# The final RMSNorm of a hybrid decoder step: its factors with tokens on the partitions, formed by a power on GpSimd

## The chip, the cores and the metric

The kernel runs on one core of a Trainium2 chip. The metric is the device time of one execution in microseconds, as a median over several runs. One execution was also taken by the hardware profiler; "the span" is the time from its first to its last instruction.

The five engines are named as in the profile: PE (TensorE, with PEld for its weight loads), DVE (VectorE), ACT (ScalarE), POOL (GpSimd) and SP (SyncE, which here only issues DMAs). Each works through its own queue in order and waits for the others through semaphores.

## The reference, cut to what matters

One layer of a decoder, for 512 prompt tokens and 8 sample tokens of 1024 features, in float32: dilated attention and a gated linear attention, then an MLP with a squared ReLU, then a last norm. The end is what the change touches:

```python
def rmsnorm(x, g):
    xf = x.astype(jnp.float32)
    y = xf * lax.rsqrt(jnp.mean(xf * xf, axis=-1, keepdims=True) + EPS)
    return (y * g.astype(jnp.float32)).astype(x.dtype)
...
    h = x + mix @ w_o
    f = jnp.square(jax.nn.relu(rmsnorm(h, g_norm2) @ w_up))
    return h + f @ w_down
...
    y_prompt = rmsnorm(xp, g_final)
    y_sample = rmsnorm(xs, g_final)
```

## The kernel before

Activations lie with features on the 128 partitions and tokens along the free dimension: a tile `B` is [128, 8, 520], 8 feature blocks by 520 tokens (512 prompt and 8 sample tokens, in two column halves of 260). Weights come as panels of 128 output features by 8 blocks of 128 input features. To keep float32 accuracy with the faster float32r matmuls, every operand is split into a high part and a low part (hi by ScalarE's Copy, lo by a subtraction on VectorE), and each product takes three passes: hi x hi, hi x lo, lo x hi (`passes`, `split_panel`, line 90 and 91). One panel is thus 8 x 3 x 2 = 48 matmuls of 128x128 weights against 260 columns, in `panel_mms` (line 124).

The order of the work on each engine is set when the program is built: a scheduler places the instructions of each engine by a simulated timeline, and PSUM banks and tiles are handed out in rotation. On the chip each engine keeps that order.

The MLP runs in four quarters of the hidden width (`qd`). In each quarter eight `w_up` panels give f, the squared ReLU, split into `fh` and `fl` (lines 982 to 986): ReLU on ScalarE into `relu`, then max(ps, 0) x relu on VectorE into `fsq`, then the split. Then eight `w_down` panels are summed into `dd`. The norm ahead of the MLP is not applied to its input. Its square, `rv` = 1 / (mean + eps), is applied behind the squared ReLU instead, since relu(s x)^2 = s^2 relu(x)^2 for a positive s. For the first three quarters `dd` is multiplied by `rv` and added to `H` in the last quarter's up loop (lines 988 and 989).

The last quarter's `w_down` product is written out by hand, with its eight panels kept in SBUF (tiles `lw`), once for each column half j (0 and 1): for each of the 8 output blocks k, 24 matmuls into a bank `mps` (line 1017), then `xo` = mps x rv (line 1020), dd += xo (line 1021), the square of dd (line 1023, ACT), the running sum of squares `acc` (line 1025, all but the last square), and dd times the final norm's weight (line 1026, ACT). Behind the eight blocks come the half's norm factors: a sum over the partitions by a matmul with a matrix of ones, for `acc` (line 1028) and for the last square (line 1029), which leaves the sum on every partition; then `rsqrt` (lines 184 to 189): Ln and Exp on ScalarE and one Newton step on VectorE, on 128x260 each; then four products of two blocks each with the factors (line 1034) and their DMAs to `yT` (line 1036).

The banks `mps`, `r2`, `r3` of this part come from a pool of four PSUM banks (`bank`). On GpSimd's queue stand 42 DMAs that copy the attention caches to the outputs (line 167), paced by the matmuls.

Of the kernel before, what the change touches and what calls it, by code (L numbers as in the profile page):

```python
# [9 lines left out]
F32 = mybir.dt.float32  # L10
F32R = mybir.dt.float32r
U8 = mybir.dt.uint8
AF = mybir.ActivationFunctionType
ALU = mybir.AluOpType
# [4 lines left out]
D = 1024  # L19
S = 512  # L20
NB = 8
P = 128
HC = 260
NT = 2 * HC
KT = 8
EPS = 1e-6
# [14 lines left out]
def halves(t):  # L41
    return t.rearrange("p (j c) -> p j c", j=2)


class Build:
# [751 lines left out]
    def run(self):  # L797
        nc, tc, I, O = self.nc, self.tc, self.I, self.O
# [56 lines left out]
        p = aps.enter_context(pool("ap"))  # L855
# [73 lines left out]
        with pool("late") as p:  # L929
            for x in range(2):  # L930
                for k, ps in enumerate(self.panel_mms(oah, oal, 4), 4 * x):
                    ga = halves(gA[:, k])
                    for o, i in ((ga[:, 0], ps[0]), (ga[:, 1], ps[1])) if isinstance(ps, list) else ((ga, ps),):
                        nc.vector.tensor_tensor(o, i, o, op=ALU.mult)
            mh, ml = self.big("mh", F32R), self.big("ml", F32R)
            H = self.big("H")
            nc.sync.dma_start(H, I["xT"])
            for k in range(KT):
                ps = self.panel_mm(obh, obl)
                nc.vector.tensor_tensor(halves(gB[:, k]), ps, halves(gB[:, k]), op=ALU.mult)  # L940
                nc.vector.tensor_tensor(gA[:, k], gA[:, k], gB[:, k], op=ALU.add)
                nc.scalar.activation(mh[:, k], gA[:, k], AF.Copy)
                nc.vector.tensor_tensor(ml[:, k], gA[:, k], mh[:, k].bitcast(F32), op=ALU.subtract)
                self.pace(1)
            hh, hl = self.big("hh", F32R), self.big("hl", F32R)
            acc = p.tile([P, NT], F32, tag="acc", name="acc")
            for k in range(KT):
                ps = self.panel_mm(mh, ml)
                nc.vector.tensor_tensor(halves(H[:, k]), ps, halves(H[:, k]), op=ALU.add)
                nc.scalar.activation(hh[:, k], H[:, k], AF.Copy, scale=self.g("n2", k))  # L950
                nc.vector.scalar_tensor_tensor(hl[:, k], H[:, k], self.g("n2", k), hh[:, k].bitcast(F32),
                                               op0=ALU.mult, op1=ALU.subtract)
                if k == 0:
                    nc.scalar.activation(acc, H[:, k], AF.Square)
                else:
                    sq = p.tile([P, NT], F32, tag="sq", name="sq", bufs=2)
                    nc.scalar.activation(sq, H[:, k], AF.Square)
                    nc.vector.tensor_tensor(acc, acc, sq, op=ALU.add)
                self.pace(1)
            rv = p.tile([P, NT], F32, tag="rv", name="rv")  # L960
            self.rawp, self.rawb = p, 3
            fh, fl = self.big("fh", F32R), self.big("fl", F32R)
            dd = self.big("dd")
            for qd in range(4):
                if qd == 3:
                    flat = lambda t: t.rearrange("p a b -> p (a b)")[:, :4 * D].rearrange("p (i k n) -> p i k n", i=4, k=KT)
                    n0 = len(self.panels) - KT
                    wd = [[flat(self.big(f"lw{x}", F32R)) for x in range(2)]]
                for k in range(KT):
                    if qd == 3 and k == KT - 1:  # L970
                        for i in range(4):
                            self.wdst[n0 + i] = (wd[0][0][:, i], wd[0][1][:, i])
                    ps = self.panel_mm(hh, hl)
                    if qd == 0 and k == 0:
                        for j in range(2):
                            pr = self.bank("r2")
                            nc.tensor.matmul(pr[:, :HC], self.ones, acc[:, j * HC:(j + 1) * HC], start=True, stop=True)
                            nc.vector.tensor_scalar(rv[:, j * HC:(j + 1) * HC], pr[:, :HC], 1 / D, EPS,
                                                    op0=ALU.mult, op1=ALU.add)
                        nc.vector.reciprocal(rv, rv)  # L980
                    t = p.tile([P, NT], F32, tag="relu", name="relu", bufs=2)
                    nc.scalar.activation(halves(t), ps, AF.Relu)
                    f = p.tile([P, NT], F32, tag="fsq", name="fsq", bufs=2)
                    nc.vector.scalar_tensor_tensor(halves(f), ps, 0.0, halves(t), op0=ALU.max, op1=ALU.mult)
                    nc.scalar.activation(fh[:, k], f, AF.Copy)
                    nc.vector.tensor_tensor(fl[:, k], f, fh[:, k].bitcast(F32), op=ALU.subtract)
                    if qd == 3:
                        nc.vector.tensor_tensor(dd[:, k], dd[:, k], rv, op=ALU.mult)
                        nc.vector.tensor_tensor(dd[:, k], dd[:, k], H[:, k], op=ALU.add)
                    self.pace(1)  # L990
                if qd == 3:
                    break
                for k in range(KT):
                    ps = self.panel_mm(fh, fl)
                    dv = halves(dd[:, k])
                    if qd == 0:
                        nc.vector.tensor_copy(dv, ps)
                    else:
                        nc.vector.tensor_tensor(dv, ps, dv, op=ALU.add)
                    self.pace(1)  # L1000
            self.pace(1000)
            wd.append([flat(self.big(f"lw{2 + x}", F32R)) for x in range(2)])
            for i in range(4):
                self.wdst[n0 + 4 + i] = (wd[1][0][:, i], wd[1][1][:, i])
            for j in range(2):
                cc = slice(j * HC, (j + 1) * HC)
                for k in range(KT):
                    i = n0 + k
                    if j == 0:
                        if i + 2 < len(self.panels):  # L1010
                            self.load_panel(i + 2)
                        if i + 1 < len(self.panels):
                            self.split_panel(i + 1)
                    ps = self.bank("mps")[:, :HC]
                    for kk in range(KT):
                        for n, (w, x) in enumerate(self.passes(self.split[i], kk, fh, fl)):
                            nc.tensor.matmul(ps, w, x[:, kk, cc], start=(kk == 0 and n == 0),  # L1017
                                             stop=(kk == KT - 1 and n == 2))
                    t = p.tile([P, NT], F32, tag="relu", name="xo", bufs=2)[:, :HC]
                    nc.vector.tensor_tensor(t, ps, rv[:, cc], op=ALU.mult)  # L1020
                    nc.vector.tensor_tensor(dd[:, k, cc], dd[:, k, cc], t, op=ALU.add)
                    sq = p.tile([P, NT], F32, tag="sq", name="sq", bufs=2)[:, :HC]
                    nc.scalar.activation(sq if k else acc[:, cc], dd[:, k, cc], AF.Square)
                    if 0 < k < KT - 1:
                        nc.vector.tensor_tensor(acc[:, cc], acc[:, cc], sq, op=ALU.add)
                    nc.scalar.activation(dd[:, k, cc], dd[:, k, cc], AF.Copy, scale=self.g("fin", k))
                pr = self.bank("r3")
                nc.tensor.matmul(pr[:, :HC], self.ones, acc[:, cc], start=True, stop=False)
                nc.tensor.matmul(pr[:, :HC], self.ones, sq, start=False, stop=True)
                rs = p.tile([P, HC], F32, tag="rs3", name="rs3", bufs=2)  # L1030
                self.rsqrt(p, rs, pr[:, :HC], HC, 1 / D)
                for k in range(0, KT, 2):
                    ks = slice(k, k + 2)
                    nc.vector.tensor_tensor(dd[:, ks, cc], dd[:, ks, cc], rs.unsqueeze(1).to_broadcast([P, 2, HC]),
                                            op=ALU.mult)
                    nc.sync.dma_start(O["yT"][:, ks, cc], dd[:, ks, cc])

# [145 lines left out]
```

## Time and profile before

| | us |
|---|---|
| median of 3 runs | 938.59 (937.89 to 943.15) |
| profiled execution | 939.2 |
| its span | 937.4 |
| PE busy | 920.3 (98% of the span), 8306 matmuls |
| DVE, ACT, POOL busy | 549.0, 380.0, 67.4 |

In a row of a timeline or chain the first number is the start in us from the span's start, the second the duration in us. In a row of groups, "x4 | 0.8, 198" is the count, the busy time in us and the mean duration in ns. A busy PE is not a PE at its peak, since matmuls overlap: the busy time of one matmul in a stream is longer than its distance to the next. Idle time in brackets names the engine whose work ended the wait.

### The profile page before, as it was taken

Reading aid. Unit: us, or ns where it says so; the run is one execution under the profiler, and the core shown is the slowest. Engines: PE = TensorE matmul, PEld = TensorE weight load, DVE = VectorE, ACT = ScalarE, POOL = GpSimd, SP = SyncE. Lnnn points to the kernel's source line nnn. Section 1 sums busy time; section 2 is a strip of 40 time slices with the busy share of each in tenths; the row PEclk is TensorE's granted clock in tenths of the full one; section 3 lists DMA queues with packets and bytes.
Section 4 is the critical chain, followed back from the end, with each engine's and each line's share of the span. In section 5 each row is a group of like instructions: output and inputs, shape, how many; then the busy total and the mean of one; then the engine's idle time right before and its main releaser. Section 6 shows DMA issues by size and latency. Waiting matters only on the chain.

```text
span 937.4 us, 19831 instructions
## 1 busy us (share of the span) xinstructions
PE 920.3 (98%) x8306; PEld 896.3 (96%) x8306; DVE 549.0 (59%) x1078; ACT 380.0 (41%) x735; POOL 67.4 (7%) x119
## 2 busy tenths in 40 slices
PE   9899999999999999999999999999999999999995
PEld 9899999999998999989999999999999999999995
DVE  7757566665766949586855556433443345555654
ACT  6133423443645536565633443322432243224432
POOL 1000000000201112010000000010000000000000
PEclk9899999999999999999999999999999999999998
DMA  6365454233444444222677767777865232323301
GB/s 245 114 237 181 142 191 155 101 131 116 166 150 165 128 165 144 69 74 69 235 278 277 272 226 269 270 269 270 294 254 175 96 93 87 104 92 106 121 30 63
DMA packets 37147, 155.27 MB, mean 166 GB/s; under 512 B 5129, under 2 KB 11537, under 8 KB 35106
## 3 DMA queue, kind: packets, MB, share of 16 engines
q1 hardware_dynamic: 32066, 95.26, 29.8%
q0 software_dynamic: 4848, 58.73, 18.0%
q8 instruction: 65, 1.06, 0.5%
q14 instruction: 24, 0.20, 0.1%
q10 hardware_dynamic: 144, 0.01, 0.0%
HBM read 140.66 MB, written 54.17 MB: 208 GB/s over the span
## 4 chain that ended last, share of the span: by engine, by line
PE 95%; DVE 2%; DMA 1%; issue 1%; ACT 0%; SPq 0%; DVEq 0%; ACTq 0%
PE mps L124 80%; PE mps L1017 5%; PE pvp L383 1%; PE lev L583 1%; PE gpo L670 1%; PE vps L318 1%; PE ptp L368 1%; PE gpu L674 1%; PE sps L352 1%; DMA xr<-in_xT 1%; PE gso L737 1%; PE gpo L672 1%; PE sps L347 1%; PE mps L547 0%; PE zp L592 0%
## 5 line engine op out<-in xcount | busy, mean ns | idle before, releaser
L90 ACT ACTIVATE whi<-raw 128x512 fp32r<-128x512 f32 x264 | 165.7, 630 | 358.6 <-PE mps L124 325.6
L91 DVE TENSOR_TENSOR wlo<-raw,whi 128x512 fp32r<-128x512 f32 x264 | 183.4, 695 | 152.2 <-ACT whi L90 149.9
L124 PE MATMUL mps<-uh,whi 128*128 128x260 f32 x928 | 194.0, 288 | 3.0 <-DVE rt L281 3.0
L124 PE MATMUL mps<-ul,whi 128*128 128x260 f32 x928 | 194.3, 288 | 0.2 <-DVE ul L219 0.2
L124 PE MATMUL mps<-uh,wlo 128*128 128x260 f32 x928 | 191.5, 286 | 0.0
L124 PEld LDWEIGHTS mps<-uh,whi 128*128 128x128 f32 x928 | 144.6, 190 | 6.1 <-issue 5.5
L124 PEld LDWEIGHTS mps<-ul,whi 128*128 128x128 f32 x928 | 145.2, 190 | 3.1 <-issue 1.7
L124 PEld LDWEIGHTS mps<-uh,wlo 128*128 128x128 f32 x928 | 144.7, 189 | 1.2 <-issue 0.8
L124 PE MATMUL mps<-hh,wlo 128*128 128x260 f32 x512 | 103.2, 283 | 0.0
L124 PE MATMUL mps<-hh,whi 128*128 128x260 f32 x512 | 103.2, 283 | 0.0
L124 PE MATMUL mps<-hl,whi 128*128 128x260 f32 x512 | 103.0, 283 | 0.0
L124 PEld LDWEIGHTS mps<-hh,whi 128*128 128x128 f32 x512 | 79.0, 188 | 0.1
L124 PEld LDWEIGHTS mps<-hh,wlo 128*128 128x128 f32 x512 | 79.0, 188 | 0.0
L124 PEld LDWEIGHTS mps<-hl,whi 128*128 128x128 f32 x512 | 78.7, 188 | 0.0
L124 PE MATMUL mps<-fh,wlo 128*128 128x260 f32 x384 | 77.3, 283 | 0.0
L124 PE MATMUL mps<-fl,whi 128*128 128x260 f32 x384 | 77.2, 283 | 0.0
L124 PE MATMUL mps<-fh,whi 128*128 128x260 f32 x384 | 76.8, 282 | 0.0
L124 PEld LDWEIGHTS mps<-fh,wlo 128*128 128x128 f32 x384 | 59.2, 188 | 0.0
L124 PEld LDWEIGHTS mps<-fl,whi 128*128 128x128 f32 x384 | 59.0, 188 | 0.0
L124 PEld LDWEIGHTS mps<-fh,whi 128*128 128x128 f32 x384 | 59.0, 188 | 0.0
L1017 PE MATMUL mps<-fh,lw 128*128 128x260 f32 x256 | 46.6, 283 | 0.0
L1017 PEld LDWEIGHTS mps<-fh,lw 128*128 128x128 f32 x256 | 39.6, 188 | 0.1
(336 smaller groups left out, 1301.1 us busy)
## 6 DMA issues: line engine op xcount, KB each, us to landing
raw<-in_w_in SPq DMA_DIRECT2D x57, 512.0 KB, 3.3
raw<-in_w_up SPq DMA_DIRECT2D x32, 512.0 KB, 4.0
raw<-in_w_down SPq DMA_DIRECT2D x32, 512.0 KB, 5.2
sx<-in_state SPq DMA_DIRECT2D x8, 512.0 KB, 4.9
sx<-dV SPq DMA_DIRECT2D x8, 512.0 KB, 4.7
out_sgla<-sx POOLq DMA_DIRECT2D x8, 512.0 KB, 5.7
raw<-in_w_pb SPq DMA_DIRECT2D x8, 512.0 KB, 5.5
raw<-in_w_o SPq DMA_DIRECT2D x8, 512.0 KB, 5.5
```

What stands on the lines that cost most here:

```text
L90: nc.scalar.activation(hi, raw[:, x:x + n], AF.Copy)
L91: nc.vector.tensor_tensor(lo, raw[:, x:x + n], hi.bitcast(F32), op=ALU.subtract)
L124: self.last = nc.tensor.matmul(out[j], w, x[:, k, j * HC:(j + 1) * HC], start=(k == 0 and n == 0), stop=(k == kt - 1 and n == 2))
L318: nc.tensor.transpose(pt[:, r * P:(r + 1) * P], vt[:, r * P:(r + 1) * P], self.c["ident"])
L347: nc.tensor.matmul(pss[hh][:, hp, first * P:], Q[rows, hp, b * P:(b + 1) * P], K[rows, hp, (b - 1 + first) * P:(b + 1) * P], start=True, s ...
L352: nc.tensor.matmul(pss[hh][:, hp, gg * P:(gg + 1) * P], Q[rows, i, b * P:(b + 1) * P], K[rows, i, b * P:(b + 1) * P], start=True, stop=True)
L368: nc.tensor.transpose(pt[:, hh, x], prs[hp][:, hh, x * P:(x + 1) * P], self.c["ident"])
L383: nc.tensor.matmul(po[64 * hh:64 * hh + 64, hp * P:(hp + 1) * P], v, pTs[hp][:, hh, x], start=(x == first), stop=(x == 1))
L583: self.nc.tensor.matmul(ps[32 * i:32 * i + 32, c], k[:, 32 * b:32 * b + 32], q[:, n * b:n * b + n], start=True, stop=True)
L670: nc.tensor.matmul(po[:, :256], ST[:, c], V[:, c], start=True, stop=(c == 0))
L672: nc.tensor.matmul(po[:, :256], qe[:, c * P:(c + 1) * P], st, start=False, stop=True)
L1017: nc.tensor.matmul(ps, w, x[:, kk, cc], start=(kk == 0 and n == 0), stop=(kk == KT - 1 and n == 2))
```

## The change

Three edits, all in the last quarter and the final norm.

In the last quarter's activations VectorE forms `relu` as max(ps, 0) x rv, in place of ScalarE's ReLU, so that `fsq` is already multiplied by `rv`. The last `w_down` product then needs no multiplication by `rv`: `xo` is gone, and dd is the sum of the bank and dd.

In the final norm the sums over features are formed with tokens on the partitions: the squares are the stationary operand (65 tokens at a time, four times 65 = 260) and one column of ones the moving one, so that the sums of a half come out as a 65x4 tile. For `acc` and for the last square these are four matmuls each. VectorE scales and adds eps on 65x4. GpSimd raises to the power of -0.5 (against a tile `half` filled with -0.5, set once). Four matmuls spread the factors: the column of 65 factors, repeated over 128 columns, is the stationary operand and the identity the moving one, so that each partition gets the factors of all 260 tokens, in PSUM.

The scalings read the factors from PSUM, in five pieces of 1, 2, 2, 2 and 1 blocks, with a DMA each.

```diff
-                    nc.scalar.activation(halves(t), ps, AF.Relu)
+                    if qd == 3:
+                        nc.vector.scalar_tensor_tensor(halves(t), ps, 0.0, halves(rv), op0=ALU.max, op1=ALU.mult)
+                    else:
+                        nc.scalar.activation(halves(t), ps, AF.Relu)
...
+            half = p.tile([65, 4], F32, tag="half", name="half")
+            nc.gpsimd.memset(half, -0.5)
...
-                    t = p.tile([P, NT], F32, tag="relu", name="xo", bufs=2)[:, :HC]
-                    nc.vector.tensor_tensor(t, ps, rv[:, cc], op=ALU.mult)
-                    nc.vector.tensor_tensor(dd[:, k, cc], dd[:, k, cc], t, op=ALU.add)
+                    nc.vector.tensor_tensor(dd[:, k, cc], ps, dd[:, k, cc], op=ALU.add)
...
-                pr = self.bank("r3")
-                nc.tensor.matmul(pr[:, :HC], self.ones, acc[:, cc], start=True, stop=False)
-                nc.tensor.matmul(pr[:, :HC], self.ones, sq, start=False, stop=True)
-                rs = p.tile([P, HC], F32, tag="rs3", name="rs3", bufs=2)
-                self.rsqrt(p, rs, pr[:, :HC], HC, 1 / D)
-                for k in range(0, KT, 2):
-                    ks = slice(k, k + 2)
-                    nc.vector.tensor_tensor(dd[:, ks, cc], dd[:, ks, cc], rs.unsqueeze(1).to_broadcast([P, 2, HC]),
-                                            op=ALU.mult)
-                    nc.sync.dma_start(O["yT"][:, ks, cc], dd[:, ks, cc])
+                pr, rs = self.bank("r3"), p.tile([65, 4], F32, tag="rs3", name="rs3", bufs=2)
+                for t in range(4):
+                    tt = slice(j * HC + 65 * t, j * HC + 65 * t + 65)
+                    nc.tensor.matmul(pr[:65, t:t + 1], acc[:, tt], self.ones[:, :1], start=(t == 0), stop=False)
+                for t in range(4):
+                    nc.tensor.matmul(pr[:65, t:t + 1], sq[:, 65 * t:65 * t + 65], self.ones[:, :1], start=False, stop=(t == 3))
+                nc.vector.tensor_scalar(rs, pr[:65, :4], 1 / D, EPS, op0=ALU.mult, op1=ALU.add)
+                nc.gpsimd.tensor_tensor(rs, rs, half, op=ALU.pow)
+                pb = self.bank("r4")[:, :HC]
+                for t in range(4):
+                    nc.tensor.matmul(pb[:, 65 * t:65 * t + 65], rs[:, t:t + 1].to_broadcast([65, P]),
+                                     self.c["ident"][:65, :65], start=True, stop=True)
+                for a, b in ((0, 1), (1, 3), (3, 5), (5, 7), (7, 8)):
+                    nc.vector.tensor_tensor(dd[:, a:b, cc], dd[:, a:b, cc],
+                                            pb.unsqueeze(1).to_broadcast([P, b - a, HC]), op=ALU.mult)
+                    nc.sync.dma_start(O["yT"][:, a:b, cc], dd[:, a:b, cc])
```

The edits move lines by up to ten: the products are at L1022 in the changed kernel (L1017 before), dd's sum at L1024, the sums at L1034 and L1036, scale and eps at L1037, the power at L1038, the spreading at L1041, the scalings at L1044.

The scheduler places the new instructions. On TensorE, at the seam between the two column halves (lw_10634 are the first half's last panels, lw_10100 the panels with which the second half begins), stood before, around the sum over `acc`:

```order
L1017 MATMUL mps<-fl,lw_10634 128x260
L1017 MATMUL mps<-fh,lw_10635 128x260
L1028 MATMUL r_10930<-acc,ones 128x260
L1017 MATMUL mps<-fh,lw_10100 128x260
L1017 MATMUL mps<-fl,lw_10100 128x260
```

and 29 products further on, inside the second product group of the second half, the sum over the last square:

```order
L1017 MATMUL mps<-fh,lw_10100 128x260
L1017 MATMUL mps<-fl,lw_10100 128x260
L1029 MATMUL r_10930<-sq,ones 128x260
L1017 MATMUL mps<-fh,lw_10101 128x260
L1017 MATMUL mps<-fh,lw_10100 128x260
```

Now the same place on TensorE reads, with all three groups of the norm in one piece (r_10916 holds the sums, rs_10917 the factors, r_10928 the spread factors):

```order
L1022 MATMUL mps<-fl,lw_10634 128x260
L1022 MATMUL mps<-fh,lw_10635 128x260
L1034 MATMUL r_10916<-ones,acc 65x1 x4
L1036 MATMUL r_10916<-ones,sq 65x1 x4
L1041 MATMUL r_10928<-ident,rs_10917 128x65 x4
L1022 MATMUL mps<-fh,lw_10100 128x260
```

The sum over the last square has moved ahead of the whole second half, and the spreading, which reads the power's result, stands there too.

On VectorE the first half's norm stood before among the second half's first additions (r_10930 the sums, rs_10933 the factors):

```order
L185 TENSOR_SCALAR rv<-r_10930 128x260
L187 TENSOR_TENSOR ra<-rs_10933 128x260
L188 SCALAR_TENSOR_TENSOR ra<-ra,rv 128x260
L1020 TENSOR_TENSOR xo<-mps,rv 128x260
L189 SCALAR_TENSOR_TENSOR rs_10933<-ra,rs_10933 128x260
L1021 TENSOR_TENSOR dd<-dd,xo 128x260
L1034 TENSOR_TENSOR dd<-dd,rs_10933 128x2x260 x4
```

and now between the first half's last addition and the second half's first ones:

```order
L1024 TENSOR_TENSOR dd<-mps,dd 128x260
L1037 TENSOR_SCALAR rs_10917<-r_10916 65x4
L1044 TENSOR_TENSOR dd<-dd,r_10928 128x260
L1044 TENSOR_TENSOR dd<-dd,r_10928 128x2x260 x3
L1044 TENSOR_TENSOR dd<-dd,r_10928 128x260
L1024 TENSOR_TENSOR dd<-mps,dd 128x260 x2
```

No addition of the second half stands ahead of the first half's scalings any more.

At the end of GpSimd's queue the difference of the two orders is this; the memset of `half` stands further up, ahead of the cache copies:

```order
 L167 DMA out_ca3k<-in_ca3k 16x16384 x16
 L167 DMA out_ca3v<-in_ca3v 16x16384 x16
-L1164 UNCONDITIONAL_BRANCH
-L1164 ISA
+L1038 TENSOR_TENSOR rs_10917<-rs_10917,half 65x4
+L1038 TENSOR_TENSOR rs_11182<-rs_11182,half 65x4
+L1174 UNCONDITIONAL_BRANCH
+L1174 ISA
```

The two powers, one for each half, are GpSimd's last work, behind the copies.

## The prediction

> **What bounds the kernel now.** I read the page's chain of work that ended last, then the same chain from 900 us on, then the timeline of the last matmuls and what follows them. In the chain's shares by engine, the first line of that part, TensorE holds nearly everything:
>
> ```profile
> PE 95%; DVE 2%; DMA 1%; issue 1%; ACT 0%; SPq 0%; DVEq 0%; ACTq 0%
> ```
>
> So a microsecond in which TensorE stands still counts in full, and work of VectorE, ScalarE or GpSimd counts only where TensorE waits for it, or after the last matmul. The chain from 900 us on (start, duration, what) shows the seam between the two column halves of the last product:
>
> ```profile
> 899.98 2.64 PE mps L1017 x22
> 902.62 0.44 PE r L1028 x2
> 903.06 3.44 PE mps L1017 x29
> 906.50 0.44 PE r L1029 x2
> 906.94 19.40 PE mps L1017 x163
> ```
>
> The first half's products end at 902.62. Its column sums (L1028, L1029) are two short pieces between products of the second half, and TensorE never waits: they cost it 2 x 0.44 = 0.88 us. The second half ends at 906.94 + 19.40 = 926.34, with 19.40 / 163 = 0.119 us a product. The timeline of what follows (start, duration, engine, operation, tiles, in brackets the idle time before):
>
> ```profile
> 926.36 0.43 DVE L1020 TENSOR_TENSOR xo<-mps,rv 128x260 f32<-128x260 f32 x1 [1.04 <-PE mps L1017]
> 926.83 0.43 DVE L1021 TENSOR_TENSOR dd<-dd,xo 128x260 f32<-128x260 f32 x1
> 927.29 0.42 ACT L1023 ACTIVATE sq<-dd 128x260 f32<-128x260 f32 x1 [1.89 <-DVE dd L1021]
> 927.74 0.51 ACT L1026 ACTIVATE dd<-dd,gcols 128x260 f32<-128x260 f32 x1
> 927.76 0.30 PEld L1029 LDWEIGHTS r<-sq,ones 128*128 128x128 f32 x2 [1.41 <-ACT sq L1023]
> 927.76 0.70 PE L1029 MATMUL r<-sq,ones 128*128 128x260 f32 x2 [1.00 <-ACT sq L1023]
> 928.50 0.48 ACT L184 ACTIVATE ra<-r,eps 128x260 f32<-128x260 f32 x1 [0.25 <-PE r L1029]
> 929.01 0.42 ACT L186 ACTIVATE rs<-ra 128x260 f32<-128x260 f32 x1
> 929.01 0.43 DVE L185 TENSOR_SCALAR rv<-r 128x260 f32<-128x260 f32 x1 [1.76 <-ACT ra L184]
> 929.47 0.43 DVE L187 TENSOR_TENSOR ra<-rs 128x260 f32<-128x260 f32 x1
> 929.93 0.43 DVE L188 SCALAR_TENSOR_TENSOR ra<-ra,rv 128x260 f32<-128x260 f32 x1
> 930.39 0.43 DVE L189 SCALAR_TENSOR_TENSOR rs<-ra,rs 128x260 f32<-128x260 f32 x1
> 930.86 0.70 DVE L1034 TENSOR_TENSOR dd<-dd,rs 128x520 f32<-128x520 f32 x1
> ```
>
> This is a chain with no overlap: 926.34 to 930.86, **4.52 us**, from the last product to the first scaling of the output. After it come four scalings and the output's DMAs. The mean busy share of the DMA engines from 925 to 938 us, in 40 slices of 0.325 us, ends the picture:
>
> ```profile
> DMA  0000000000000000000000079999999970000000
> ```
>
> The output flows without a gap through ten slices (3.25 us, from about 932.5 to 935.7) and stops 1.7 us before the end, so the end is set by when this flow starts and by its bytes, not by the last scaling.
>
> **The change, part by part.** *The tail.* Write S for the time from a half's last product to the first scaling in the new form. Multiplying by rv is gone from the path: dd is formed straight from PSUM, so 0.47 us (926.36 to 926.83) falls out and the squares are ready 927.76 - 926.34 - 0.47 = 0.95 us after the last product. The rest of S has other shapes; these are the nearest rows, small products on TensorE, a narrow VectorE operation, and GpSimd's operations:
>
> ```profile
> 376.18 0.53 PEld L765 LDWEIGHTS gsr<-sqS,ones 128*128 128x128 f32 x4
> 376.29 0.53 PE L765 MATMUL gsr<-sqS,ones 128*128 128x32 f32 x4
> 157.17 0.55 PE L468 MATMUL spS<-kn,qd 128*32 128x8 f32 x12
> L185 DVE TENSOR_SCALAR rv<-ssq 128x4 f32<-128x4 f32 x4 | 0.8, 198 | 0.2 <-ACT jk L683 0.2
> 245.45 0.17 DVE L604 COPY el<-qe 128x4 f32<-128x4 f32 x1
> 245.70 1.39 POOL L605 TENSOR_TENSOR qe<-qe,QKb 128x512 f32<-128x512 f32 x1 [24.71 <-DVE el L604]
> 366.12 3.27 POOL L605 TENSOR_TENSOR qe<-qe,QKb 128x512 f32<-128x512 f32 x1 [0.17 <-DVE el L604]
> L664 POOL COPY ST<-sd 32x128 f32<-32x128 f32 x16 | 5.1, 319 | 46.2 <-DVE sd L661 43.4 <-DVE oS L753 2.3
> 0.24 0.10 POOL L1175 MEMSET const-float32-0.0<- 128x1 f32 x1 [0.24 <-issue]
> ```
>
> A float32 product runs as two instructions (L1029: one product in the code, x2 here), so each group of four products is 8. With 128 weight columns four instructions take 376.18 to 376.82, 0.64 us. Two loads of that size take 0.30 (L1029) and four 0.53, so each more adds about 0.11, and eight instructions take 0.64 + 4 x 0.11 = 1.1. With 32 columns twelve take 0.55, so eight some 0.4. The sums over sq load 65 columns: between 0.4 and 1.1, I take 0.7. The spreading loads 128 columns (rs repeated): I take 1.1, with 0.4 as the low end. The scale and eps on 65x4 take 0.20 + 0.02 by L185. From VectorE's end to GpSimd's start is 245.70 - 245.62 = 0.08; I take 0.08 for the way back to TensorE too, 0.02 on to VectorE. The power p has no row. Its low end is 0.10 (a one-column MEMSET), its high end 3.27 (the longest GpSimd two-operand row, 512 columns against 4). It has few columns but more arithmetic than a copy, so I take 0.6, about twice the COPY's 0.32: an estimate.
>
> S = 0.95 + 0.7 + 0.22 + 0.08 + 0.6 + 0.08 + 1.1 + 0.02 = **3.75 us**. The tail gains 4.52 - 3.75 = 0.77. The new split of the scalings (1, 2, 2, 2, 1 panels) starts the DMA flow about 0.27 us earlier (0.43 instead of 0.70 for the first), but with only half a piece to move while the second scaling runs for 0.70 us, so the flow then pauses for about as long; I count nothing. The queue issues five transfers instead of four, hidden behind the flow.
>
> *The seam.* The order on TensorE shows what the tail's gain costs. Before, the first half's two sums stood 29 products apart. Now the sums over acc, the sums over sq and the spreading stand directly behind each other, ahead of the second half's first product, and the spreading waits for the power. TensorE works in order, so everything behind it, the whole second half, waits for the same S. On the path that is S against 0.88 before: 3.75 - 0.88 = **+2.87 us**. The sums over acc fit into the first 0.95. VectorE's queue puts the five scalings ahead of the second half's first additions; TensorE gets going only when they begin, so they hide behind a column group of 24 x 0.119 = 2.9 us. The PSUM bank of the spread factors is wanted again by the fourth group, 8.6 us later.
>
> *The last quarter's activations.* ReLU leaves ScalarE; VectorE gets eight operations of 128x520, each 0.70 by L1034. The stage as one stretch (its columns: length, busy time and count of PE, PEld, DVE, ACT, POOL, clock, DMA) and its last steps:
>
> ```profile
> 833.00:879.40 46.40, 46.40 (x389) 46.40 (x387) 24.29 (x37) 22.26 (x39) 0.00 (x0) 1.00 0.39 126
> 886.52 0.62 ACT L985 ACTIVATE fh<-fsq 128x520 fp32r<-128x520 f32 x1
> 887.34 0.69 DVE L986 TENSOR_TENSOR fl<-fsq,fh 128x520 fp32r<-128x520 f32 x1
> ```
>
> VectorE idles 22 of 46 us; 8 x 0.70 = 5.6 fits. Only the last panel can hurt: fl is ready at 888.03, and its first reader stands 115 products ahead of L1028 in the order, at about 902.45 - 115 x 0.119 = 888.8. The cover is 0.7 us. VectorE's added 0.70 there is offset by ScalarE's ReLU leaving the same chain, so I count nothing; with the cover gone it would cost at most 0.7. The sixteen multiplications by rv vanish, hidden except for the 0.47 already counted. On GpSimd's queue the memset of the -0.5 tile stands ahead of the 42 cache copies, which nothing on the path waits for: nothing.
>
> *Sum.* +2.87 - 0.77 = **+2.1 us**, or 2S - 5.4. At the low ends (0.4, 0.4, p 0.10) S is 2.3 and the sum -0.9; at the high ones (1.1, 1.1, 3.27) S is 6.8 and the sum +8.2. The profiled execution took 939.2 us, 937.4 of span and 1.8 around it, 0.6 above the median of 938.59; the difference is applied to the median: **940.7 us**.
>
> **TensorE's clock.** The stall has a second price. These stretches of 3.41 us (columns as above) show one stall of this kernel and, last, the tail:
>
> ```profile
> 37.05:40.46 3.41, 1.41 (x12) 1.19 (x10) 3.41 (x8) 0.63 (x1) 0.00 (x0) 1.00 0.17 41
> 40.46:43.87 3.41, 2.41 (x11) 2.44 (x12) 3.41 (x10) 0.00 (x0) 0.55 (x1) 0.50 0.50 125
> 43.87:47.29 3.42, 3.42 (x18) 3.42 (x18) 0.33 (x3) 0.27 (x1) 1.07 (x2) 0.50 0.64 202
> 47.29:50.70 3.41, 3.41 (x30) 3.41 (x30) 0.81 (x2) 1.15 (x3) 0.00 (x0) 1.00 0.92 275
> 924.51:927.93 3.42, 2.42 (x19) 2.01 (x18) 1.29 (x3) 1.47 (x4) 0.00 (x0) 1.00 0.00 0
> ```
>
> After a stretch with 2.0 us idle the granted clock was 0.50 for two stretches, with 18 matmuls where a full one has 30: a loss of 3.41 x (1 - 18/30) = 1.4 us for each full stretch. After a stretch with 1.0 us idle (the last row) the clock stayed. The seam's stall has about S - 0.7 - 0.7 - 1.1 = 1.25 us in which TensorE does nothing, nearer to the 1.0 that kept the clock, if its one-column products count as work. The Trainium skill (TensorE: Matmul & The Clock Gate, Part 1, What's actually happening) says that the clock is halved after at least one idle window of about 3.4 us. By that rule the seam loses no clock and the sum stays at +2.1; the row at 37.05, with 1.41 us of work in such a window, lost it all the same, so the trace is stricter, and the loss is a rival.
>
> **The rivals.** *The clock is lost at the seam.* For it: the one-column products move next to nothing, and without those 1.4 us the idle time would be 2.6. Against it: the row of 924.51. One to two stretches at half clock, 1.4 to 2.8 us, give 942.1 to 943.5, say 942.8.
>
> *Slower: the power is slow.* Place: GpSimd's operation in both halves, once before TensorE's second half and once in the tail. At p = 3.27, S is 6.42 and the sum 2 x 6.42 - 5.4 = +7.4; a stall that long loses the clock too, some 2.1: 948.1 us. For it: no row shows a power, and GpSimd's longest two-operand row took 3.27. Against it: only four columns. It decides (over 4.7 us) from p = 1.9 with the clock kept, from 0.9 with it lost. The Trainium skill (GPSIMD Engine Reference, 2.1 Instruction dispatch) adds that the first call of a freshly loaded routine pays about 6 us without an instruction in the profile. By that figure the seam alone would grow by 6 us, an estimate of 947 us; the trace's first two-operand GpSimd row began 0.08 after its operand, and shows no such wait.
>
> *The pieces are short.* At the low ends the tail gains 2.2 us and the seam costs 1.4: 937.7 us. For it: the 32-column products ran at 0.034 us each. Against it: the spreading loads 128 columns.
>
> That the change does nothing is no rival: the order shows both edits.
>
> **How the numbers follow.** Chances: the forecast 0.46, the clock lost 0.28, the slow power 0.13, the short pieces 0.13. The bound of 0.5%, 4.7 us, is about what a measurement of this kernel can tell from no change. Faster by that much would need more than the tail's whole 4.52: 0.01. Slower: the slow power and the upper end of the lost clock, 0.17. Within: 0.82. The range runs from the short pieces' 937.7 to just above the lost clock's 943.5, 944.0, and leaves out the slow power.
>
> **What would show it.** In the changed kernel's chain: TensorE's gap at the seam, about 3.7 us, released by GpSimd (right), or no gap (the order was misread). The POOL row of the power: 0.6, and above 0.9 the slow rival gains. The granted clock behind the seam: 1.00 or 0.50. The tail from last product to first scaling: 3.75 against 4.52. A gap at the start of L1022's products would show that the ReLU edit costs. I am wrong in kind if the time falls by more than 1 us: then the seam is cheaper than the order says.

## The result, and the profile after

The changed kernel takes 945.39 us as a median of 9 runs (942.81 to 947.17), the kernel before 938.73 in the same series (937.67 to 943.15). The ratio is 1.0055, with a 95% interval of 1.0037 to 1.0073: about 5.2 us (3.5 to 6.9) slower; the two medians as they stand are 6.7 us apart, inside that interval. A second series gave 943.67 against 939.12 us, ratio 1.0052 (1.0040 to 1.0065). So it is slower; the interval reaches to both sides of the 0.5% that was set as the bound. Put on the median of 938.59 from which the forecast started, 1.0055 is 943.8 us: 3.1 above the forecast of 940.7 and just inside its upper end of 944.0. The median of the first series as it stands, 945.39, is outside.

The profiled execution took 942.81 us, the fastest of its series, with a span of 941.0. In the shares of its chain that ended last, waiting in "issue" has grown from 1% to 8%, and TensorE's share has fallen from 95%:

```profile
PE 86%; issue 8%; DMA 3%; DVE 3%; ACT 0%; SPq 0%; POOLq 0%; POOL 0%; DVEq 0%; ACTq 0%
```

The chain of the changed kernel from 875 us on (start, duration, what) shows the seam. Where two pieces of 0.44 us stood between products, a chain runs through four engines:

```profile
878.39 23.05 PE mps L1022 x192
...
901.47 0.44 DVE dd L1024
...
901.93 0.43 ACT sq L1026
...
902.40 0.65 PE r L1036 x8
...
903.07 0.17 DVE rs L1037
...
903.28 0.10 issue
903.38 1.05 POOL rs L1038
```

The first half's products now run in one piece and end at 901.44 (before, the first half ended at 902.62). The squares are ready 0.96 us later, the sums over sq take 0.65, the scale 0.17, the way to GpSimd 0.14, the power 1.05. The timeline of the same place shows how it goes on:

```profile
902.40 0.63 PE L1036 MATMUL r<-ones,sq 128*65 128x1 f32 x8 [0.55 <-ACT sq L1026]
...
904.48 1.10 PE L1041 MATMUL r<-ident,rs 65*128 65x65 f32 x8 [1.44 <-POOL rs L1038]
...
905.62 1.03 DVE L1044 TENSOR_TENSOR dd<-dd,r 128x260 f32<-128x260 f32 x2 [2.39 <-PE r L1041]
...
910.08 0.43 DVE L1024 TENSOR_TENSOR dd<-mps,dd 128x260 f32<-128x260 f32 x1 [1.88 <-PE mps L1022]
```

TensorE waits 0.55 us for the squares and 1.44 us for the power, 2.0 us in all, and S at the seam, from the last product to the first scaling, is 905.62 - 901.45 = 4.17 us. The last row is what follows: the second half's first column group ends as VectorE's addition starts at 910.08, 4.5 us after the end of the spreading, where 24 products take 2.9. The windows of the changed kernel, cut where the granted clock changes, say why (length, busy time and count of PE, PEld, DVE, ACT, POOL, then clock, DMA share, GB/s):

```profile
902.57:905.98 3.41, 1.97 (x21) 1.88 (x21) 0.52 (x3) 0.32 (x1) 1.05 (x1) 1.00 0.00 0
905.98:909.40 3.42, 3.42 (x19) 3.42 (x18) 2.22 (x5) 0.00 (x0) 0.00 (x0) 0.50 0.63 214
909.40:912.81 3.41, 3.41 (x30) 3.41 (x30) 0.43 (x1) 0.94 (x2) 0.00 (x0) 1.00 0.30 98
...
929.87:933.28 3.41, 1.52 (x21) 1.35 (x18) 0.59 (x2) 0.93 (x2) 1.01 (x1) 1.00 0.00 0
933.28:936.70 3.42, 1.34 (x7) 1.16 (x6) 2.04 (x4) 0.00 (x0) 0.00 (x0) 0.50 0.12 41
```

Behind the seam the clock is 0.50 for one stretch of 3.4 us, with 19 matmuls instead of 30. The same happens in the tail: the clock falls at 933.28, while the factors are still being spread. The tail's timeline:

```profile
930.51 0.42 ACT L1026 ACTIVATE sq<-dd 128x260 f32<-128x260 f32 x1 [1.88 <-DVE dd L1024]
...
931.89 1.01 POOL L1038 TENSOR_TENSOR rs<-rs,half 65x4 f32<-65x4 f32 x1 [27.47 <-DVE rs L1037]
932.95 1.67 PE L1041 MATMUL r<-ident,rs 65*128 65x65 f32 x8 [1.34 <-POOL rs L1038]
934.66 2.58 DVE L1044 TENSOR_TENSOR dd<-dd,r 128x260 f32<-128x260 f32 x5 [2.85 <-PE r L1041]
```

The square starts 0.48 us after the last product, as at the seam (901.93 - 901.45), so the last product ends at 930.03, and the first scaling at 934.66 is 4.63 us later; before, it took 4.52. The spreading takes 1.67 us instead of the seam's 1.10.

So the 3.6 us between the two spans (941.0 and 937.4) divide as follows. From the first half's last product to the second half's last product it was 926.34 - 902.62 = 23.72 us, and is 930.03 - 901.45 = 28.58: +4.86, which is 4.17 - 0.88 = 3.29 of standing still and 1.57 of slow products. From there to the end it was 11.06 and is 10.97. And everything up to the first half's end is 1.17 us shorter. That last gain has nothing to do with the change. Both kernels lose the clock after the early stall at 38 to 41 us, before for two stretches (rows 40.46 and 43.87 in the prediction), here for one:

```profile
38.90:42.30 3.40, 1.12 (x9) 1.15 (x10) 3.40 (x8) 0.00 (x0) 0.29 (x1) 1.00 0.41 98
42.30:45.70 3.40, 3.40 (x18) 3.40 (x17) 1.62 (x7) 0.00 (x0) 0.49 (x2) 0.52 0.64 186
```

Without this piece of luck the pair of profiles differs by 4.8 us, close to the 5.2 of the ratio.

### The profile page after: what moved, and what is told of

The parts are those of the page before. It is cut to its first block, busy times and chain, and to the rows that moved or that the text cites. A ratio compares the mean times of both kernels' runs of the same rounds, so it can differ in the third digit from the quotient of the medians.

```text
span 941.0 us, 19882 instructions
## 1 busy us (share of the span) xinstructions
PE 923.2 (98%) x8346; PEld 899.4 (96%) x8346; DVE 545.5 (58%) x1066; ACT 375.0 (40%) x723; POOL 68.4 (7%) x122
## 4 chain that ended last, share of the span: by engine, by line
PE 86%; issue 8%; DMA 3%; DVE 3%; ACT 0%; SPq 0%; POOLq 0%; POOL 0%; DVEq 0%; ACTq 0%
PE mps L124 75%; PE mps L1022 2%; DMA kcb<-in_vc 1%; PE lev L583 1%; PE gpo L670 1%; PE vps L318 1%; PE gpu L674 1%; DMA xr<-in_xT 1%; PE gso L737 1%; PE gpo L672 1%; PE pvp L383 1%; PE sps L347 1%; DMA kcb<-dq 1%; PE zp L592 0%; PE ptp L368 0%
## 5 line engine op out<-in xcount | busy, mean ns | idle before, releaser
L1022 PE MATMUL mps<-fh,lw 128*128 128x260 f32 x256 | 47.7, 288 | 0.0
L1022 PEld LDWEIGHTS mps<-fh,lw 128*128 128x128 f32 x256 | 40.9, 194 | 0.0
```

## The experiments

The theory after this reading: the loss is all at the seam, as a stand of TensorE (3.3 us) and a clock that is lost because TensorE does too little there; the tail gives back nothing, since the clock falls in it too. The rivals: the ReLU edit costs; the second half's norm costs; or the clock plays no part. Each median rests on 4 to 12 executions. "Trace sum" below is S at the seam plus S in the tail, less the 0.88 + 4.52 = 5.40 us of before.

**1. The activations' edit alone.** Old norm, new ReLU and no multiplication by rv (against the changed kernel, cut):

```diff
-                pr, rs = self.bank("r3"), p.tile([65, 4], F32, tag="rs3", name="rs3", bufs=2)
...
+                pr = self.bank("r3")
+                nc.tensor.matmul(pr[:, :HC], self.ones, acc[:, cc], start=True, stop=False)
+                nc.tensor.matmul(pr[:, :HC], self.ones, sq, start=False, stop=True)
...
+                self.rsqrt(p, rs, pr[:, :HC], HC, 1 / D)
```

> The rv edit alone, the norm as before. Theory (the loss is TensorE's stand at the seam and the halved clock behind it, both from the new norm): no stand at the seam, the tail from last product to first scaling falls from 4.52 to 4.05 us, the time 0.5 us below before (ratio 0.9995), which the intervals will hardly show. Rival (VectorE's ReLU in the last quarter delays the first products of the last product stage): a gap of TensorE before or in that stage, time above before by 1 us or more, in the extreme by the change's whole 5 us (ratio 1.005).

Measured: 940.07 us, ratio 1.0005 (0.9991 to 1.0019). The chain of this kernel has the seam of before and a tail of 928.71 - (904.78 + 19.87) = 4.06 us:

```profile
877.89 23.04 PE mps L1020 x192
900.93 0.44 PE r L1030 x2
...
904.78 19.87 PE mps L1020 x167
...
928.71 0.70 DVE dd L1036
```

The 0.47 us in the tail is there, too little to be seen in the ratio. The interval leaves room for 1.8 us of cost and no more, and the chain shows the first half's 192 products without a gap: as the cause of the loss the ReLU edit falls.

**2. The new norm, its order at the seam put back.** The first half's sums stand behind the second half's first column group, its spreading behind the second group:

```diff
+                    if j == 1 and k == 0:
+                        rs0 = sums(0, last)
+                    if j == 1 and k == 1:
+                        scale(0, rs0)
```

> The change, but the first half's sums are issued behind the second half's first column group and the spreading behind its second. Theory: the power's wait is covered by 24 products; TensorE pays only for its own work, about 1.0 us for the sums and 0.9 for the spreading against 0.88 before, the clock stays at 1.00 behind the seam, the tail is the changed kernel's 4.6. About +1.1 us over before, ratio 1.001, some 4 us below the changed kernel. Rival (the loss is the ReLU edit or the tail): ratio stays at 1.005.

Measured: 940.28 us, ratio 1.0004 (0.9986 to 1.0021). The chain of this kernel runs through the seam:

```profile
878.55 25.92 PE mps L1045 x216
904.47 0.42 PE r L1015 x8
904.88 0.49 PE r L1017 x8
```

The power still takes 1.04 us, but products run beside it. In the tail the spreading took 1.99 us at the lower clock and the first scaling began at 931.29, 4.9 us after the last product, where 4.6 were expected: the new norm, where TensorE has nothing else, is no faster than the old one.

**3. The stand kept, TensorE kept busy in it.** Six float32 products of ones x sq, their result unread, between the sums and the spreading of each half:

```diff
+                dm = self.bank("dm")
+                for t in range(6):
+                    nc.tensor.matmul(dm[:, :HC], self.ones, sq, start=True, stop=True)
```

> The change, with six float32 products of the ones with the last square (results unused, about 1.3 us) between the sums and the spreading in both halves, while the power runs. Theory (stand and clock both count): the seam's stand stays at about 4.2 us, but the clock stays at 1.00 behind it, and in the tail the spreading takes 1.1 instead of 1.7 us: about +2.9 us over before, ratio 1.003, and less spread from run to run. If the stand alone were the cost, the ratio stays at 1.005; if the clock alone were, it falls to 1.001.

Measured: 945.0 us, ratio 1.0057 (1.0037 to 1.0077). The products were mis-sized: I had reckoned with 0.22 us each, but a float32 product is two instructions, and the twelve took 2.74 us, so that the spreading waited for them and not for the power. S grew to 5.21 us in both halves; the clock stayed at 1.00 behind the seam. The trace sum, 2 x 5.21 - 5.40 = +5.0, is what was measured (5.4): a longer stand and no lost clock happen to cost what the change costs. As a test of the clock it was inconclusive, and was repeated with half the products (5).

**4. The old norm for the first half, the new one for the second.**

```diff
+                if j == 0:
+                    pr = self.bank("r3")
+                    nc.tensor.matmul(pr[:, :HC], self.ones, acc[:, cc], start=True, stop=False)
+                    nc.tensor.matmul(pr[:, :HC], self.ones, sq, start=False, stop=True)
...
+                    continue
```

> The change, but the first half's norm as before (ones, Ln, Exp, Newton step), the new norm in the second half alone. Theory: no stand and no clock loss at the seam (0.88 us of products as before), the tail about 4.6 us as in the changed kernel: within 0.3 us of before, ratio 1.000. Rival (the loss sits in the tail or in the ReLU edit): ratio 1.005.

Measured: 940.09 us, ratio 1.0004 (0.9990 to 1.0019), with a tail of 931.71 - 926.97 = 4.74 us. With the seam as before, the loss is gone; the new norm in the tail neither gains nor costs anything measurable.

**5. The stand kept, with three products.**

```diff
+                dm = self.bank("dm")
+                for t in range(3):
+                    nc.tensor.matmul(dm[:, :HC], self.ones, sq, start=True, stop=True)
```

> The change with three float32 products of ones x sq (260 columns, result unread) between the sums and the spreading of each half; the twelve instructions of the warm kernel before took 2.74 us, so six take 1.37, as long as the scale (0.17), the power (1.05) and their hops. Theory (the loss is the stand of TensorE plus a clock lost because TensorE is idle for some 2 us there): the stand stays at 4.2 us, 3.3 more than before, the granted clock stays 1.00 behind it, the first group behind the seam takes 2.9 us and not 4.5, the tail from last product to first scaling is 4.1 us and not 4.6, the spreading in it 1.1 us and not 1.67. The sum is +3.3 - 0.4 = +2.9 us, ratio about 1.003. Rival (the clock plays no part, the stand alone is the loss): like the change, ratio 1.0055.

Measured: 940.8 us, ratio 1.0028 (1.0018 to 1.0038), an interval that excludes the change's 1.0055 and holds the forecast 1.003. The timeline of this kernel:

```profile
902.76 1.56 PE L1041 MATMUL dm<-sq,ones 128*128 128x260 f32 x6
...
903.24 1.04 POOL L1038 TENSOR_TENSOR rs<-rs,half 65x4 f32<-65x4 f32 x1 [197.18 <-DVE rs L1037]
...
904.34 1.10 PE L1044 MATMUL r<-ident,rs 65*128 65x65 f32 x8
905.48 2.58 DVE L1047 TENSOR_TENSOR dd<-dd,r 128x260 f32<-128x260 f32 x5 [2.39 <-PE r L1044]
```

and its windows, the stand and what follows it, both at full clock:

```profile
901.26:904.67 3.41, 2.83 (x26) 2.22 (x24) 0.59 (x2) 0.93 (x2) 1.04 (x1) 1.00 0.00 0
904.67:908.09 3.42, 3.42 (x30) 3.42 (x30) 2.58 (x5) 0.00 (x0) 0.00 (x0) 1.00 0.28 95
```

The stand is the same as in the change (4.17 us), and in the tail the first scaling now comes at 4.07 us. The trace sum is 4.17 + 4.07 - 5.40 = +2.8 us; measured were 2.6. Adding useless work made the kernel faster, because it kept the clock. The rival without a clock falls. The times also lie closer together, 940.6 to 941.4 against 942.8 to 947.2.

**6. A multiplication in place of the power.** It leaves out the inverse root; waits and operands stay.

```diff
-                nc.gpsimd.tensor_tensor(rs, rs, half, op=ALU.pow)
+                nc.gpsimd.tensor_tensor(rs, rs, half, op=ALU.mult)
```

> The change with a multiplication in place of the power (the inverse root is left out), so that GpSimd's instruction, its 65x4 operands and all waits stay. It prices the power's arithmetic. If the 1.05 us of the row are the start and end of any GpSimd operation of two operands, the row stays near 1.0 us and the ratio at 1.0055. If they are the power's own arithmetic, the row falls to 0.2 to 0.4 us, TensorE's idle time at the seam to about 1.3 us, the stand to 3.5 us; by my theory the clock is then kept and the sum is 2 x 3.5 - 5.4 = +1.6 us, ratio about 1.002; by the rival without a clock 1.6 us less than the change, ratio about 1.004.

Measured: 941.17 us, ratio 1.0034 (1.0021 to 1.0046). The power's price was as the second expectation had it: the row falls to 0.19 us, so 0.86 of the 1.05 is the power's own work. But the clock was not kept, although TensorE idled for only 1.2 us in all. The timeline of this kernel at the seam:

```profile
903.15 0.63 PE L1036 MATMUL r<-ones,sq 128*65 128x1 f32 x8 [0.55 <-ACT sq L1026]
...
904.13 0.19 POOL L1038 TENSOR_TENSOR rs<-rs,half 65x4 f32<-65x4 f32 x1 [197.18 <-DVE rs L1037]
...
904.38 1.97 PE L1041 MATMUL r<-ident,rs 65*128 65x65 f32 x8 [0.60 <-POOL rs L1038]
906.38 2.58 DVE L1044 TENSOR_TENSOR dd<-dd,r 128x260 f32<-128x260 f32 x5 [2.41 <-PE r L1041]
```

Its windows, cut where the clock changes (columns as above):

```profile
900.73:904.14 3.41, 2.50 (x29) 2.33 (x27) 0.59 (x2) 0.96 (x3) 0.01 (x1) 1.00 0.00 0
904.14:907.56 3.42, 3.18 (x15) 3.18 (x16) 1.18 (x3) 0.00 (x0) 0.18 (x1) 0.51 0.00 0
907.56:910.97 3.41, 3.41 (x17) 3.41 (x17) 1.40 (x3) 0.00 (x0) 0.00 (x0) 0.50 0.88 298
```

Here the clock fell after a window in which TensorE had been busy for 2.50 of 3.41 us, and stayed down after one in which it was busy for 3.18. My theory said "idle"; that fell. The theory that was left: instructions that move few columns (1.2 us of one-column sums in the first window, 2 us of spreading in the second) do not count. Run 9 tests it. The stand came out no shorter than the change's, 906.38 - 902.19 = 4.19 us, because the spreading ran at half the clock. The ratio lies between the two forecasts, 1.002 and 1.004, and does not decide between them; and the profiled execution, at 943.04 us, is the slowest of the five, so that the others may have lost less.

**7. A second power** (by 1, so that the result stays) behind the first:

```diff
+            nc.gpsimd.memset(one, 1.0)
...
                 nc.gpsimd.tensor_tensor(rs, rs, half, op=ALU.pow)
+                nc.gpsimd.tensor_tensor(rs, rs, one, op=ALU.pow)
```

> The change with a second power (by 1) behind the first, the result kept: GpSimd's part is doubled. Both theories: the stand at the seam grows by about 1.05 us to 5.2 us and the tail by as much. Theory with the clock: TensorE's idle time at the seam grows from 2 to 3 us, the clock is lost for one to two windows of 3.4 us, and the sum is the change's +5.2 us plus 2.1 plus at most another 1.5, ratio 1.008 to 1.0095. Rival without a clock: the change plus 2.1 us, ratio 1.008. If GpSimd's power were not on the path, 1.0055.

Measured: 946.51 us, ratio 1.0087 (1.0073 to 1.0101). The chain of this kernel:

```profile
901.97 0.02 issue
...
903.90 1.05 POOL rs L1040
...
905.02 1.02 POOL rs L1041
...
906.09 1.97 PE r L1044 x8
908.06 24.96 PE mps L1024 x192
933.02 0.02 issue
...
939.04 0.42 DVE dd L1047
```

The stand is 6.1 us and the tail 6.0, a trace sum of +6.7; the clock is 0.50 from about 905.3 to 912.1, two windows, of which 4.0 us lie behind the stand and cost some 1.6 by the rate of 18 matmuls for 30. Together 8.3 us, against 8.2 measured. The interval holds the forecasts with the clock and without it, so the clock's part is read from the trace alone. The power is on the path in both halves.

**8. The early stall filled.** The kernel of run 1 with nine float32 products of ones x ones behind the first panel of V, where all kernels of this case wait (cut):

```diff
-            vt = self.scaled(self.mm(), "vt", nt >= 2)
+            ps = self.mm()
+            if nt == 0:
+                dm = self.bank("dm")
+                for _ in range(9):
+                    nc.tensor.matmul(dm[:, :P], self.ones, self.ones, start=True, stop=True)
+            vt = self.scaled(ps, "vt", nt >= 2)
```

> The edit of the last quarter's activations alone with the old norm (which measured 1.0005), and nine float32 products of ones x ones (128 columns, result unread, about 0.28 us each, 2.5 us) on TensorE in the early stand at 38.4 to 41.4 us, where every kernel of this case waits 3.0 us for VectorE and loses the clock for one to two windows. Theory (the granted clock follows what TensorE does in a window of 3.4 us, and a lost window costs 1.4 to 1.6 us): the clock stays 1.00 from 41 to 47 us, 1.5 to 2.8 us are gained, ratio about 0.998, and the spread of the times narrows. Rival (the clock there has another cause, or the products delay the panel behind them by what they save): ratio 1.0005 or above.

Measured: 936.94 us, ratio 0.9987 (0.9978 to 0.9996), 936.6 to 938.7 in eleven runs. It is the one kernel here that is faster than the kernel before, by 1.2 us (0.4 to 2.1). Against run 1, whose edits it shares, it is 1.7 us by the two ratios, whose intervals just overlap. The products themselves waited 1.78 us for their PSUM bank, and still the clock stayed at 1.00 behind the stall, as the windows of this kernel show:

```profile
38.99:42.40 3.41, 1.93 (x17) 1.96 (x18) 3.41 (x9) 0.12 (x1) 0.00 (x0) 1.00 0.37 88
42.40:45.82 3.42, 3.42 (x31) 3.42 (x31) 2.02 (x7) 0.60 (x1) 0.55 (x1) 1.00 0.64 185
```

That every kernel loses the clock at this stall was too wide: run 3's profile keeps it there (last section). Here the filling did it: with a wait of 3.0 us and no filling the first of these windows would have held only about 0.7 us of products, an estimate from 42.40 - (38.69 + 3.0), where 38.69 is the end of the last product ahead of the stall.

**9. The stand filled with one-column products.** As run 5, with six products of one column instead of three of 260:

```diff
-                for t in range(3):
-                    nc.tensor.matmul(dm[:, :HC], self.ones, sq, start=True, stop=True)
+                for t in range(6):
+                    nc.tensor.matmul(dm[:, :1], self.ones, sq[:, :1], start=True, stop=True)
```

> The kernel with three float32 products of 260 columns between the sums and the spreading (clock kept, ratio 1.0028), with six products of one column (ones x the first column of sq, result unread) in their place: twelve instructions, about 0.11 us each by the weight loads, 1.3 us. They fill the same time on TensorE with instructions that move next to nothing. Theory (the granted clock follows the columns that TensorE moves, so that products of one column count as idle): the clock behind the seam falls to 0.50 for one or two windows of 3.4 us, as in the change; the spreading in the tail takes 1.7 to 2.0 us; ratio 1.0045 to 1.0065. Rival (the clock follows whether TensorE has instructions at all): the clock stays 1.00, the spreading takes 1.1 us, ratio about 1.003.

**10. The change once more**, on the same chip.

> The change as it is, once more, on the same chip and against the same runs of the kernel before as the run with one-column products. Theory: ratio 1.0045 to 1.0065, and the same as with one-column products within the intervals. Rival (one-column products keep the clock): above the run with one-column products by about 0.0025.

Measured: with one-column products 944.06 us, ratio 1.0059 (1.0045 to 1.0074); the change 943.67, ratio 1.0052 (1.0040 to 1.0065), against the same runs of the kernel before. The two are the same within their intervals, and run 5's 1.0028, measured on another chip against the kernel before on that chip, lies outside both intervals. The timeline of run 9, TensorE's instructions in the stand:

```profile
903.30 1.48 PE L1041 MATMUL dm<-sq,ones 128*128 128x1 f32 x12
...
904.89 1.10 PE L1044 MATMUL r<-ident,rs 65*128 65x65 f32 x8
```

Its windows around the loss of the clock:

```profile
903.38:906.79 3.41, 3.31 (x30) 3.22 (x29) 0.92 (x3) 0.00 (x0) 1.04 (x1) 1.00 0.00 0
906.79:910.20 3.41, 3.41 (x18) 3.41 (x17) 1.82 (x4) 0.00 (x0) 0.00 (x0) 0.50 0.75 255
```

In the first window TensorE is busy for 3.31 of 3.41 us, with as many instructions as a full window (30), and the clock is lost all the same: they were one-column products, then the spreading with 65 columns, and full products only at the end. So neither the number of instructions nor the busy time decides, and products that move one column do not hold the clock. The count of moved columns does not decide either: run 5 kept the clock in its window at 901.26 with little else than six instructions of 260 columns, 1560 in all, and run 9 lost it at the early stall with 13 such instructions, 3380 columns. What the rows of these runs have in common is how long wide products, of 128 columns or more, run; no run here measured that apart.

In run 9's tail the spreading took 1.46 us, less than the 1.7 to 2.0 expected, since the clock fell at 934.09, while it was running.

## Why the prediction was right and wrong

**Right: what the change does.** The whole first norm has become a stand of TensorE ahead of the second half; the ReLU edit costs nothing that run 1 can show; the memset, the cover of the last panel and the five transfers cost nothing: the first half's 192 products run without a gap, and the last stage is 10.97 us against 11.06.

**The terms of S.** Forecast and measured, at the seam: the way to the squares 0.95 and 0.95; the sums over sq 0.7 and 0.65; the scale 0.22 and 0.17; the spreading 1.1 and 1.10; the hops together 0.18 and some 0.25. The step that failed by size is "I take 0.6, about twice the COPY's 0.32" for the power: it took 1.05. The power alone would make S 4.20 instead of 3.75; it measured 4.17, and the seam +3.29 instead of +2.87. The 6 us of a first call, which the prediction took from the Trainium skill (GPSIMD Engine Reference, 2.1 Instruction dispatch), did not show: the first power took 1.05 us, the second 1.01, and the first began 0.15 us after its operand.

**Wrong: the likeliest case.** The step reads "nearer to the 1.0 that kept the clock, if its one-column products count as work". They do not (run 9), and so the likeliest case, a stand with the clock kept, is not what happened: the time falls into the range because its upper end was set by the lost clock, a rival. The stretch that I counted as 1.25 us of idle time was, for the clock, the whole stand of over 3 us less the products at its edges. The rival "the clock is lost at the seam", to which I gave 0.28, is what happened. Its price of 1.4 to 2.8 us was about right: 1.57 in the profiled run. Its total of 942.8 was too low by the two other terms: the power's 0.45, in both halves, and the slow spreading in the tail.

**Wrong: the tail's gain.** "The tail gains 4.52 - 3.75 = 0.77" took the clock in the tail for granted. There the small products leave the clock's window as empty as at the seam, it falls while the factors are being spread, and the spreading takes 1.67 us (1.99 in run 2). S is 4.63 and the gain -0.1. With the clock held it is 4.07 (run 5), a gain of 0.45, and that is no more than the edit of the activations gives with the old norm (4.06, run 1): the new norm itself gains nothing in the tail.

**The sum by the measured terms** is +3.29 at the seam, +0.11 in the tail to the first scaling and +1.57 for the clock: +5.0 us, against 5.2 (3.5 to 6.9) by the ratio. Behind the first scaling 0.2 us are made up, as the last stage of 10.97 against 11.06 shows; so the two spans give 4.8. The slow-power rival was to decide "from 0.9 with it lost", and p is 1.05 with the clock lost: the two rivals met half way, at the bound. Taking them as exclusive gave "slower" 0.17; their common ground, a power a little over 0.9 and a lost clock, should have been a case of its own.

What stays open: how many windows the change loses in a run that was not profiled. The two series' 14 runs of it lie from 942.8 to 947.2 with granted clocks of 0.992 down to 0.988, and the slower ones have the lower clocks; one or two windows more at half clock, each 0.0018 of the mean clock, would fit that. But only the fastest run of each series was seen from inside. The second one, of 943.1 us, agrees with the first: a stand of 905.47 - 901.29 = 4.18 us, one window lost behind it and one at the early stall, and 1.98 us for the spreading in the tail.

## What to carry to other kernels

A norm between two halves of a product is nearly free as long as its pieces stand between products; put in one piece, its whole latency is a stand of the busiest engine, and here 3.3 us of it cost another 1.6 in clock. Matmuls that move one column did not hold the clock here, and the spreading, with 65 columns, took 1.1 us with the clock held and up to 2.0 without, so the durations of small matmuls must not be taken from a dense stage. Where a stall can't be avoided, wide products whose result nobody reads can fill it: that was worth 2.3 us at the seam and in the tail (ratios 1.0052 and 1.0028), and 1.2 us at the early stall, with run 1's edits.

## What the runs showed of the hardware

- The clock's changes lie on a grid. In the changed kernel's profile the clock falls at 905.98 and 933.28, 27.30 us apart, which is 8 x 3.41; each stretch at 0.50, but for the last, which lasts to the end, is 3.41 us long or twice that. The Trainium skill (TensorE: Matmul & The Clock Gate, Part 1, What's actually happening) describes a free-running window of 3413 ns; the traces agree, and the first fall lies elsewhere in each, at 40.46 in the kernel before and at 43.22 in run 9. It has the clock halved after at least one idle window; here a window that was 97% busy by the profile (903.38 in run 9) lost it.
- How full a window must be shows at the early stall, where TensorE stands for 3.0 us and runs nothing but products of 260 columns around it. The windows there in run 9 and then in run 3, cut where the clock can change:

```profile
39.80:43.22 3.42, 1.54 (x13) 1.57 (x14) 3.42 (x7) 0.00 (x0) 0.55 (x1) 1.00 0.46 110
43.22:46.63 3.41, 3.41 (x18) 3.41 (x17) 1.20 (x6) 0.61 (x2) 0.68 (x2) 0.50 0.60 176
...
41.93:45.34 3.41, 1.72 (x14) 1.75 (x15) 3.41 (x9) 0.00 (x0) 0.55 (x1) 1.00 0.42 100
45.34:48.76 3.42, 3.42 (x31) 3.42 (x30) 1.72 (x7) 1.12 (x2) 0.86 (x2) 1.00 0.63 185
```

- With 1.54 us of wide products, 45% of the window, the clock was lost; with 1.72, 50%, it was kept. So the same stall costs a different number of windows by where it falls on the grid: two in the profile of the kernel before, one in the change's, none in run 3's. In run 6, with the shorter wait for GpSimd, the seam cost two where the change lost one. An estimate from these rows: the change's stand has 905.39 - 901.45 = 3.94 us without wide products, so of two windows, 6.83 us, 2.89 are left, and the emptier one has at most 1.44; it would be lost wherever the stand falls.
- Not every series of small matmuls loses the clock. In run 3's window from 417.40 to 420.81 TensorE was busy for 2.01 us with 78 matmuls, most of them of 16 to 64 columns, and the clock stayed at 1.00. How few columns are too few stays open between that and the one-column products of run 9.
- On GpSimd a 65x4 float32 multiplication took 0.19 us and a power 1.05; an exponent of 1 took as long (1.02) as one of -0.5.
- Eight float32 instructions that load 65 weight columns and move one took 0.63 us; with 128 weight columns and 65 moved 1.10 at full clock and 1.97 at half.
